# A trunk of two decoder layers on one core: all four output projections in panels of 1024 channels, with 60 of 136 chunk pairs by seven block products

## The chip, the core and the metric

The kernel runs on one core of a Trainium2 chip. The metric is the device time of one execution in microseconds, the median of several runs. The core has a matrix engine (TensorE, PE in the profile), three engines for elementwise work (VectorE, DVE; ScalarE, ACT; GpSimd, POOL) and a queue that issues the transfers (SyncE, SP). Each engine works through its own queue in order; semaphores hold an instruction until what it needs is there.

## The reference

256 tokens of 2048 channels pass through two layers, all in float32. Each layer is a mixer and a gated feed-forward block, both with a residual sum, and a last RMS norm closes the trunk:

```python
def reference(x, ...):
    h = x
    for i in range(DEPTH):                       # 2
        hn = rms_norm(h, mix_norm[i])
        if i % N_MIXERS == 0:
            h = h + retention_mixer(hn, ...)     # ends in y @ w_out, 4096 -> 2048
        else:
            h = h + moba_mixer(hn, ...)          # ends in o @ w_out, 2048 -> 2048
        h = h + conv_ffn(rms_norm(h, ffn_norm[i]), ...)   # ends in (silu(gate) * val) @ w_down, 5632 -> 2048
    return rms_norm(h, final_norm)
```

The four products that end the four blocks are the output projections. Their inner lengths are 4096, 5632, 2048 and 5632, that is 32, 44, 16 and 44 chunks of 128.

## The kernel before

**A product in three passes.** Each float32 factor is split into a high part (rounded to the fp32r type by ScalarE) and a low part (the difference, by VectorE); a product is high times high, high times low and low times high, three matmuls that are summed in PSUM. The split of the activations is stored with them (`hT`, `yT`, `oT`, `actT`: first 256 columns the high part, next 256 the low part). The weights come from memory in units of 1 MB (`raw`, 128 x 2048 elements, four buffers) and are split here, in parts of up to 1024 columns: ScalarE writes `wh` (L185) and VectorE writes `wl` (L186), four buffers each.

**The order of work.** The program is a list of parts. While TensorE works on part i, the parts up to i + 3 (`LOOKAHEAD`) may be split, and a buffer of `wh` is free again when TensorE is through with the part four places earlier. Work that hangs on a finished sum (residual sum, transposes, norms) is put some parts later with `after`. Within these rules a scheduler sets the order on each engine.

**Output projections before.** In `panel_a` a panel has 512 output channels; for each chunk and each half t of the tokens (128 tokens) three matmuls of 512 columns run (L265 to L267). A part is two chunks, 12 matmuls; two chunks with 1024 channels would be 24. Retention and block attention each take four such panels (`out_proj`, with `residual` adding the sum to `h`).

**Sevens and eights.** The first panel of each feed-forward projection is `panel_s`, with 1024 channels. Two chunks, two halves of the tokens and two halves of the channels make a product of 2 x 2 blocks by 2 x 2 blocks. As eight block products (an *eight* below) a pair is 8 x 3 = 24 matmuls in two parts, L354. As seven block products (a *seven*) it is 21 matmuls in four parts of 6, 3, 6 and 6 matmuls; for that the weights need three sums of blocks beside the blocks themselves (L203 to L205, on VectorE, in place in `raw`), and all that is used must be split: 3584 columns in place of 2048. The activations need sums of blocks too, the forms (L365 to L369, split at L185 and L186 into `hT`, which is free at that time). Seven of the 22 pairs of this panel are sevens, each with two eights between it and the next:

```python
SEVEN = list(range(3, NFB // 2, 3))
```

The sums of a seven are combined from four PSUM banks into `h` in `residual_s` (L739).

Of the kernel before, what the change touches and what calls it, by code (L numbers as in the profile page):

```python
# [28 lines left out]
SEVEN = list(range(3, NFB // 2, 3))  # L29
# [40 lines left out]

def build(tc, a, out):
# [27 lines left out]
    rB = cst.tile([P, S], F32, name="rB")  # L99
    rBq = cst.tile([P, S], F32, name="rBq")  # L100
# [53 lines left out]
    def issue_split(i):  # L154
# [3 lines left out]
        while state["dma"] <= min(u + 2, len(units) - 1):  # L158
            issue_dma(state["dma"])
            state["dma"] += 1  # L160
        wh = whi.tile([P, 1024], F32R, name="wh")
        wl = wlo.tile([P, 1024], F32R, name="wl")
        if i == 0:
            r = raws[u]

            def split(sl):
                split_to(wh[:, sl], wl[:, sl], r[:, sl])

            def rest():
                x_T(2, 2)  # L170
                split(slice(512, 1024))
                for _ in range(LOOKAHEAD):
# [21 lines left out]
    def split_b21(raw, wh, wl):  # L194
        split_to(wh[:, :512], wl[:, :512], raw[:, 1024:1536])

    def split_b11_b22(raw, wh, wl):
        b, h4, l4 = (v.rearrange("p (b n) -> p b n", n=512) for v in (raw, wh, wl))
        split_to(h4, l4, b[:, 0:4:3, :])

    def split_u4_u2(raw, wh, wl):
        b = raw.rearrange("p (b n) -> p b n", n=512)
        dve.tensor_tensor(b[:, 0:2, :], b[:, 0:4:3, :], b[:, 1:2, :].to_broadcast([P, 2, 512]), op=ALU.add)  # L203
        dve.tensor_tensor(b[:, 3, :], b[:, 0, :], b[:, 3, :], op=ALU.add)
        dve.tensor_tensor(b[:, 2, :], b[:, 3, :], b[:, 2, :], op=ALU.add)  # L205
        split_to(wh, wl, raw[:, 1024:])
# [50 lines left out]
    def panel_a(w, nk, n0, xT, done, before=None, split_last=0):  # L257


        box, late, items = {}, [], []  # L260

        def mm_t(t, k, c, wh, wl):
            acc, xt = box["acc"][t], xT[0]
# [5 lines left out]
        for k0 in range(0, nk, 2):  # L269
            def mm(wh, wl, k0=k0):  # L270
                if k0 == 0:
                    if before is not None:
                        before()
                    if split_last:
                        box["acc"] = [pacc.tile([P, 2, 512], F32, name="acc")[:, 0, :] for _ in range(2)]
                    else:
                        acc = pacc.tile([P, 2, 512], F32, name="acc")
                        box["acc"] = [acc[:, 0, :], acc[:, 1, :]]
                        box["tile"] = acc
                if k0 >= nk - 2 * split_last:  # L280
                    late.append((k0, wh, wl))
                    for c in range(2):
                        mm_t(0, k0 + c, c, wh, wl)
                else:
                    for c in range(2):
                        for t in range(2):
                            mm_t(t, k0 + c, c, wh, wl)
                if k0 == nk - 2:
                    if not split_last:
                        return finish(done, box["tile"])  # L290
                    done(box["acc"][0], 0)
                    for kl, wh, wl in late:
# [37 lines left out]
    def panel_s(w, nk, n0, xT, seven, forms, done):  # L330
# [3 lines left out]
        pairs = nk // 2  # L334
        acc, count, uses, items = {}, {}, {}, []
        for c in range(pairs):
            for b, m in (((2, 1), (3, 1), (4, 1), (1, 1), (5, 1), (6, 1), (7, 1)) if c in seven else
                         ((2, 2), (3, 2), (4, 2), (8, 2))):
                uses[b] = uses.get(b, 0) + 3 * m

        def bank(b):
            if b not in acc:
                if b in (2, 3, 4, 8):
                    acc[b] = paux.tile([P, 512], F32, name="aux")
                else:
                    i, j = (1, 6) if b in (1, 6) else (5, 7)
                    t = pacc.tile([P, 2, 512], F32, name="acc")
                    acc[i], acc[j] = t[:, 0, :], t[:, 1, :]
            return acc[b]
# [9 lines left out]
        def fs(s, i):  # L359
            return forms[:, 2 * s, i * P : (i + 1) * P], forms[:, 2 * s + 1, i * P : (i + 1) * P]  # L360

        def make_forms(s, k):

            a, f = ffn["p1"].tile([P, 2, S], F32, name="af", tag="bs"), ffn["p1"].tile([P, 4, P], F32, name="ff", tag="u1")
            dve.tensor_tensor(a, xT[0][:, k : k + 2, :S].bitcast(F32), xT[0][:, k : k + 2, S:].bitcast(F32), op=ALU.add)  # L365
            a4 = a.rearrange("p c (t m) -> p (c t) m", m=P)
            dve.tensor_tensor(f[:, 0:2, :], a4[:, 1:2, :].to_broadcast([P, 2, P]), a4[:, 0:4:3, :], op=ALU.subtract)
            dve.tensor_tensor(f[:, 2, :], a4[:, 0, :], f[:, 1, :], op=ALU.subtract)
            dve.tensor_tensor(f[:, 3, :], a4[:, 2, :], f[:, 2, :], op=ALU.subtract)  # L369
            f = f.rearrange("p f m -> p (f m)")  # L370
            split_to(forms[:, 2 * s, :], forms[:, 2 * s + 1, :], f)

        for c in range(pairs):
            k, last = 2 * c, c == pairs - 1
            ahead = (seven.index(c + 1), k + 2) if c + 1 in seven else None
            if c in seven:
                s = seven.index(c)

                def b21(wh, wl, k=k, last=last):
                    mul(2, xs(0, k + 1), wh[:, 0, :], wl[:, 0, :])  # L380
                    if last:
                        done(2, acc[2])

                def b11_b22(wh, wl, k=k, s=s, last=last):
                    mul(1, xs(0, k), wh[:, 0, :], wl[:, 0, :])
                    mul(3, fs(s, 3), wh[:, 1, :], wl[:, 1, :])
                    if last:
                        done(3, acc[3])

                def u4_u2(wh, wl, k=k, s=s, last=last):  # L390
                    mul(4, xs(1, k + 1), wh[:, 0, :], wl[:, 0, :])
                    mul(6, fs(s, 2), wh[:, 1, :], wl[:, 1, :])
                    if last:
                        for b in (1, 6, 4):
                            done(b, acc[b])

                def u1_u3(wh, wl, s=s, last=last):
                    mul(5, fs(s, 1), wh[:, 0, :], wl[:, 0, :])
                    mul(7, fs(s, 0), wh[:, 1, :], wl[:, 1, :])
                    if last:  # L400
                        for b in (5, 7):
                            finish(lambda acc, b=b: done(b, acc), acc[b])
# [598 lines left out]
```

## Time and profile before

| | |
|---|---|
| time, median of 3 runs | 2610.46 us (2609.38 to 2610.65) |
| profiled execution: its time, its span | 2611.6 us, 2609.8 us |
| busy share of the span: TensorE, VectorE, ScalarE | 99%, 67%, 51% |
| granted clock of TensorE, mean | 0.999 |
| chain that ended last | TensorE 97% |

The span is from the first to the last instruction of the profiled execution; its time also holds what lies around the program. A busy share is a mean over the whole span, and stages differ. The start to start distance of two instructions on an engine that never waits is what one costs; the durations in a row are longer, since neighbours overlap.

### The profile page before, as it was taken

The numbers are of one execution on the slowest core, as the hardware profiler recorded it, in microseconds if no ns is written. First come the engines' busy times: TensorE is split into PE (matmuls) and PEld (weight loads), VectorE is DVE, ScalarE is ACT, GpSimd is POOL, SyncE is SP. The second block draws the span as 40 slices with busy tenths as digits, with TensorE's granted clock in tenths as the row PEclk, the third lists the DMA queues.
The fourth block names the chain that finished last, engine by engine and source line by source line (L and its number), as shares of the span: only waits on it lengthen the run. The fifth ranks groups of instructions, "written<-read, shape, count | busy, mean of one in ns | idle before, by whom it ended". The sixth has DMA issues, their size and how long they took to land.

```text
span 2609.8 us, 33769 instructions
## 1 busy us (share of the span) xinstructions
PE 2595.9 (99%) x13456; PEld 2209.7 (85%) x13456; DVE 1758.9 (67%) x2247; ACT 1329.6 (51%) x1713; POOL 10.2 (0%) x24
## 2 busy tenths in 40 slices
PE   9999999999999999999999999999999999999998
PEld 7888888888888888888788888888888888888887
DVE  6666656564557777777975466665677777779764
ACT  5444444444445555555554454454555555555543
POOL 0000000000000000000000000000000000000000
PEclk9999999999999999999999999999999999999999
DMA  7655555555555555555555655555555565555563
GB/s 269 229 189 182 179 177 178 182 189 178 193 185 186 194 189 184 192 193 183 178 205 195 205 189 179 173 190 173 182 191 185 190 194 186 186 194 178 193 226 129
DMA packets 361149, 493.87 MB, mean 189 GB/s; under 512 B 8080, under 2 KB 258976, under 8 KB 360736
## 3 DMA queue, kind: packets, MB, share of 16 engines
q1 hardware_dynamic: 355248, 483.52, 56.1%
q10 hardware_dynamic: 5744, 8.20, 1.0%
q8 instruction: 105, 1.72, 0.3%
q14 instruction: 52, 0.43, 0.0%
HBM read 489.57 MB, written 5.27 MB: 190 GB/s over the span
## 4 chain that ended last, share of the span: by engine, by line
PE 97%; DVE 1%; issue 0%; ACT 0%; DMA 0%; SPq 0%; POOLq 0%; POOL 0%; DVEq 0%; ACTq 0%
PE acc L317 34%; PE acc L320 17%; PE acc L265 12%; PE acc L267 12%; PE acc L266 12%; PE aux L354 6%; PE acc L354 1%; PE aux L431 1%; PE aux L422 1%; PE aux L423 1%; PE aux L421 1%; DVE wl L186 0%; ACT wh L185 0%; PE aux L923 0%; DMA h<-in_x_dram 0%
## 5 line engine op out<-in xcount | busy, mean ns | idle before, releaser
L186 DVE TENSOR_TENSOR wl<-raw,wh 128x1024 fp32r<-128x1024 f32 (+1 forms) x941 | 1137.4, 1215 | 776.9 <-ACT wh L185 764.0
L185 ACT ACTIVATE wh<-raw 128x1024 fp32r<-128x1024 f32 (+1 forms) x941 | 985.3, 1053 | 1156.4 <-PE acc L317 477.3
L317 PE MATMUL acc<-hT,wh 128*128 128x512 f32 x3840 | 1209.6, 396 | 1.4 <-DVE hT L437 1.4
L320 PEld LDWEIGHTS acc<-hT,wl 128*128 128x128 f32 x3840 | 721.7, 188 | 170.1
L320 PE MATMUL acc<-hT,wl 128*128 128x256 f32 x3840 | 755.5, 278 | 0.0
L317 PEld LDWEIGHTS acc<-hT,wh 128*128 128x128 f32 x3840 | 587.0, 189 | 3.8 <-DVE hT L437 1.6
L265 PE MATMUL acc<-wh,hT 128*128 128x512 f32 x640 | 251.0, 392 | 0.7 <-DVE bs L567 0.7
L267 PE MATMUL acc<-wh,hT 128*128 128x512 f32 x640 | 249.3, 390 | 0.0
L266 PE MATMUL acc<-wl,hT 128*128 128x512 f32 x640 | 249.3, 390 | 0.0
L354 PE MATMUL aux<-wh,actT 128*128 128x512 f32 x536 | 170.2, 390 | 0.3 <-ACT wh L185 0.2
L718 DVE SCALAR_TENSOR_TENSOR t<-u,cw,t 128x256 f32<-128x256 f32 x352 | 146.8, 479 | 0.0
L267 PEld LDWEIGHTS acc<-wh,hT 128*128 128x128 f32 x640 | 120.2, 188 | 25.3
L265 PEld LDWEIGHTS acc<-wh,hT 128*128 128x128 f32 x640 | 120.2, 188 | 24.6 <-DVE bs L567 0.9
L266 PEld LDWEIGHTS acc<-wl,hT 128*128 128x128 f32 x640 | 120.3, 188 | 23.7
L265 PE MATMUL acc<-wh,actT 128*128 128x512 f32 x352 | 137.2, 390 | 0.0
L266 PE MATMUL acc<-wl,actT 128*128 128x512 f32 x352 | 137.1, 389 | 0.0
L267 PE MATMUL acc<-wh,actT 128*128 128x512 f32 x352 | 137.0, 389 | 0.0
L354 PEld LDWEIGHTS aux<-wh,actT 128*128 128x128 f32 x536 | 100.6, 188 | 22.0 <-ACT wh L185 1.9
L354 PE MATMUL aux<-wl,actT 128*128 128x512 f32 x268 | 105.7, 395 | 0.0
L265 PE MATMUL acc<-wh,yT 128*128 128x512 f32 x256 | 100.0, 390 | 0.0
L267 PE MATMUL acc<-wh,yT 128*128 128x512 f32 x256 | 99.7, 389 | 0.0
L266 PE MATMUL acc<-wl,yT 128*128 128x512 f32 x256 | 99.6, 389 | 0.0
(162 smaller groups left out, 1925.5 us busy)
## 6 DMA issues: line engine op xcount, KB each, us to landing
raw<-in_ffn_w_up_dram SPq DMA_DIRECT2D x176, 1024.0 KB, 5.1
raw<-in_ret_w_in_dram SPq DMA_DIRECT2D x93, 1024.0 KB, 5.2
raw<-in_ffn_w_down_dram SPq DMA_DIRECT2D x88, 1024.0 KB, 5.4
raw<-in_moba_w_qkv_dram SPq DMA_DIRECT2D x48, 1024.0 KB, 5.2
raw<-in_ret_w_out_dram SPq DMA_DIRECT2D x32, 1024.0 KB, 5.0
raw<-in_moba_w_out_dram SPq DMA_DIRECT2D x16, 1024.0 KB, 5.0
skewD<-tblD ACTq DMA_DIRECT2D x1, 3072.0 KB, 13.2
raw<-in_ret_w_in_dram SPq DMA_DIRECT2D x5, 512.0 KB, 9.1
```

What stands on the lines that cost most here:

```text
L185: act.activation(hi, src, AF.Copy)
L186: dve.tensor_tensor(lo, src, hi.bitcast(F32), op=ALU.subtract)
L265: pe.matmul(acc, lhsT=xh, rhs=wh[:, c, :], start=(k == 0), stop=False)
L266: pe.matmul(acc, lhsT=xh, rhs=wl[:, c, :], start=False, stop=False)
L267: pe.matmul(acc, lhsT=xl, rhs=wh[:, c, :], start=False, stop=(k == nk - 1))
L317: pe.matmul(acc[:, b, :], lhsT=wh[:, c, b * P : (b + 1) * P], rhs=xt[:, k, :], start=(k == 0), stop=False)
L320: pe.matmul(acc[:, b, S:], lhsT=wl[:, c, b * P : (b + 1) * P], rhs=xt[:, k, :S], start=False, stop=(k == KC - 1))
L354: pe.matmul(bank(b), lhsT=xs, rhs=ws, start=(n == 1), stop=(n == uses[b]))
L421: pe.matmul(dst, lhsT=lh, rhs=rh, start=start, stop=False)
L422: pe.matmul(dst, lhsT=lh, rhs=rl, start=False, stop=False)
L423: pe.matmul(dst, lhsT=ll, rhs=rh, start=False, stop=stop)
L718: dve.scalar_tensor_tensor(t[:, i, :], u[:, i, tap : tap + S], c[:, tap, b : b + 1], t[:, i, :], op0=ALU.mult, op1=ALU.add)
```

## The change

All four output projections become two panels of 1024 channels. Which pairs are sevens, in which order they come, and where forms are made or taken again is written out:

```python
FFN_SEQS = wide_seqs([5, 8, 10, 12, 14, 17, 19, 21], [1, 3, 7, 15], "AASSASFSASFSASFSAFAAAA")
RET_SEQS = wide_seqs([5, 7, 9, 11, 13, 15], [2, 4], "AASSASFSASFSAAAA")
MOB_SEQS = wide_seqs([3, 5, 7], [], "AASSSAAA")
```

The first list names the sevens of the first panel; in the string for the second panel, A is an eight, S a seven with a form that the first panel left in `hT`, F a seven whose form is made anew. That is 8 and 12 sevens of 22 and 22 pairs in each feed-forward projection, 6 and 8 of 16 and 16 in retention, 3 and 3 of 8 and 8 in block attention: 60 of 136, where 14 were before. The parts of a seven come in another order, and the sums of the weights are made with the first and the second part (L223, L228, L229). The sums of a seven stay in PSUM until they are added to `h`. `rB` and `rBq` become halves of one tile that also serves as a temporary. At the start, two parts are split ahead instead of three for the first eight parts, and transfers are issued one unit ahead instead of two. The end keeps its form: the last four parts finish the first 128 tokens ahead of the second 128.

```diff
-SEVEN = list(range(3, NFB // 2, 3))
...
+def wide_seqs(first, fresh, second):
+    n = len(second)
+    one = [(p, first.index(p) if p in first else None, p in first) for p in range(n)]
+    again, new = list(enumerate(first)), list(enumerate(fresh))
+    others = [p for p in range(n) if p not in first and p not in fresh]
+    two = []
+    for c in second:
+        if c == "A":
+            two.append((others.pop(0), None, False))
+        else:
+            slot, p = (again if c == "S" else new).pop(0)
+            two.append((p, slot, c == "F"))
+    return one, two
...
-        while state["dma"] <= min(u + 2, len(units) - 1):
+        while state["dma"] <= min(u + (1 if i < 8 else 2), len(units) - 1):
...
+    def split_b11_b22(raw, wh, wl):
+        b = blocks(raw)
+        split_to(blocks(wh), blocks(wl), b[:, 0:4:3, :])
+        dve.tensor_tensor(b[:, 0:2, :], b[:, 0:4:3, :], b[:, 1:2, :].to_broadcast([P, 2, 512]), op=ALU.add)
+
     def split_b21(raw, wh, wl):
...
+        b = blocks(raw)
+        split_to(wh[:, :512], wl[:, :512], b[:, 2, :])
         dve.tensor_tensor(b[:, 3, :], b[:, 0, :], b[:, 3, :], op=ALU.add)
         dve.tensor_tensor(b[:, 2, :], b[:, 3, :], b[:, 2, :], op=ALU.add)
...
-            while state["split"] <= min(i + LOOKAHEAD if i else 0, n - 1):
+            ahead = 0 if i == 0 else 2 if i < 8 else LOOKAHEAD
+            while state["split"] <= min(i + ahead, n - 1):
...
+        def opens(i):
+
+            if i == 0:
+                if before is not None:
+                    before()
+                begin()
+            if i == sevens[0]:
+                begin_sevens()
+            if i + 2 < len(seq) and seq[i + 2][2]:
+                make_forms(seq[i + 2][1], 2 * seq[i + 2][0])
+
+        def seven(i, k, s):
+            def b11_b22(wh, wl):
+                opens(i)
+                mul(1, xs(0, k), wh[:, 0, :], wl[:, 0, :])
+                mul(3, fs(s, 3), wh[:, 1, :], wl[:, 1, :])
+                give()
+
+            def b21(wh, wl):
+                mul(2, xs(0, k + 1), wh[:, 0, :], wl[:, 0, :])
+                give()
+
+            def u1_u3(wh, wl):
+                mul(5, fs(s, 1), wh[:, 0, :], wl[:, 0, :])
+                mul(7, fs(s, 0), wh[:, 1, :], wl[:, 1, :])
+                give()
+
+            def u4_u2(wh, wl):
+                mul(4, xs(1, k + 1), wh[:, 0, :], wl[:, 0, :])
+                mul(6, fs(s, 2), wh[:, 1, :], wl[:, 1, :])
+                ends()
+
+            return [(split_b11_b22, b11_b22), (split_b21, b21), (0, u1_u3), (1, u4_u2)]
...
-    def out_proj(w, nk, xT, g0, use_r, j0=0):
+    def out_proj(w, seqs, xT, temps, g0, use_r):
...
+        emit(panel_s(w, 0, xT, seqs[0], temps, residual_s(0, temps)))
+        emit(panel_s(w, 1024, xT, seqs[1], temps,
+                     residual_s(2, temps, lambda: [transpose_first(i) for i in range(2)], rest)))
...
-        emit(panel_s(wd, NFB, 0, actT, SEVEN, hT, residual_s(0, then)))
-        if last:
-            emit(panel_a(wd, NFB, 2 * 512, actT, last_done(2)))
-            emit(panel_a(wd, NFB, 3 * 512, actT, last_half, split_last=3))
-        else:
-            out_proj(wd, NFB, actT, g_next, use_next, j0=2)
+        if not last:
+            return out_proj(wd, FFN_SEQS, actT, temps_ffn, g_next, use_next)
...
+        emit(panel_s(wd, 0, actT, FFN_SEQS[0], temps_ffn, residual_s(0, temps_ffn)))
+        emit(panel_s(wd, 1024, actT, FFN_SEQS[1], temps_ffn, residual_s(2, temps_ffn, last=last_bank), end=4,
+                     before=gains_first))
```

The first place is VectorE's queue between sevens in the feed-forward projection of layer 0. Before, late in the panel with sevens (`wl` at L186 is the low part of a split, the three lines on `raw` are the sums of a seven):

```order
L186 TENSOR_TENSOR wl<-raw,wh 128x512
L186 TENSOR_TENSOR wl<-raw,wh 128x1024
L203 TENSOR_TENSOR raw<-raw 128x1024
L204 TENSOR_TENSOR raw<-raw 128x512
L205 TENSOR_TENSOR raw<-raw 128x512
L186 TENSOR_TENSOR wl<-raw,wh 128x1024 x6
L186 TENSOR_TENSOR wl<-raw,wh 128x512
```

The same engine after, in the second panel, in the stretch S A S F of the string (`wl` is now L208, `hT<-ff` the split of a form):

```order
L208 TENSOR_TENSOR wl<-raw,wh 128x1024 x5
L208 TENSOR_TENSOR wl<-raw,wh 128x512
L223 TENSOR_TENSOR raw<-raw 128x1024
L208 TENSOR_TENSOR hT<-ff,hT 128x512
L228 TENSOR_TENSOR raw<-raw 128x512
L208 TENSOR_TENSOR wl<-raw,wh 128x1024
L229 TENSOR_TENSOR raw<-raw 128x512
L208 TENSOR_TENSOR wl<-raw,wh 128x1024 x2
L208 TENSOR_TENSOR wl<-raw,wh 128x512
L223 TENSOR_TENSOR raw<-raw 128x1024
L228 TENSOR_TENSOR raw<-raw 128x512
L229 TENSOR_TENSOR raw<-raw 128x512
```

Before, eight splits stand between one group of sums and the next, four of them those of two eights; after, the seven behind the eight has its sums interleaved with the split of a form, and the next group of sums stands only three splits behind, with no eight between.

The second place is VectorE's queue where the first panel of that projection ends and the next one begins. Before (`m` are copies of the sums of a seven in SBUF, made by ScalarE):

```order
L739 TENSOR_TENSOR h<-aux,h 128x512
L186 TENSOR_TENSOR wl<-raw,wh 128x1024 x2
L739 TENSOR_TENSOR h<-h,m_10977 128x512
L739 TENSOR_TENSOR m_10979<-m_10979,m_10977 128x512
L186 TENSOR_TENSOR wl<-raw,wh 128x1024
L739 TENSOR_TENSOR m_10977<-m_10979,m_10996 128x512
L186 TENSOR_TENSOR wl<-raw,wh 128x1024
L739 TENSOR_TENSOR h<-h,m_10977 128x512
L739 TENSOR_TENSOR m_10979<-m_10979,m_10994 128x512
L186 TENSOR_TENSOR wl<-raw,wh 128x1024
L739 TENSOR_TENSOR h<-h,m_10979 128x512
L739 TENSOR_TENSOR m_10996<-m_10977,m_10994 128x512
```

After (`acc` and `aux` are PSUM):

```order
L558 TENSOR_TENSOR rBs<-acc,m 128x512
L208 TENSOR_TENSOR wl<-raw,wh 128x1024
L558 TENSOR_TENSOR h<-h,rBs 128x512
L223 TENSOR_TENSOR raw<-raw 128x1024
L558 TENSOR_TENSOR m<-acc,m 128x512
L208 TENSOR_TENSOR wl<-raw,wh 128x512
L558 TENSOR_TENSOR h<-h,m 128x512
L228 TENSOR_TENSOR raw<-raw 128x512
L558 TENSOR_TENSOR rBs<-acc,rBs 128x512
L229 TENSOR_TENSOR raw<-raw 128x512
L558 TENSOR_TENSOR h<-h,rBs 128x512
L208 TENSOR_TENSOR wl<-raw,wh 128x1024 x3
```

The sums into `h` stood between splits of plain parts; now the last of them stand between the weight sums of the second panel's first seven.

## Rows read from the trace of the kernel before

**Rows 1.** The page of the profile: the busy time of each engine, the granted clock in 40 slices, and the share of the span that each engine has in the chain that ended last.

```profile
PE 2595.9 (99%) x13456; PEld 2209.7 (85%) x13456; DVE 1758.9 (67%) x2247; ACT 1329.6 (51%) x1713; POOL 10.2 (0%) x24
...
PEclk9999999999999999999999999999999999999999
...
PE 97%; DVE 1%; issue 0%; ACT 0%; DMA 0%; SPq 0%; POOLq 0%; POOL 0%; DVEq 0%; ACTq 0%
```

**Rows 2.** Busy time of each engine by stretch: in the feed-forward projection of layer 0 the pairs around the first three sevens, the rest of that panel, and what stands behind it (a panel of 512 channels and a part of the next). Columns: stretch and its length, then busy us (instructions) for PE, PEld, DVE, ACT, POOL, the granted clock, DMA share and GB/s.

```profile
1262.00:1302.00 40.00, 39.35 (x167) 30.66 (x166) 38.30 (x53) 23.18 (x26) 0.00 (x0) 1.00 0.48 164
1302.00:1364.00 62.00, 62.00 (x272) 50.31 (x271) 46.21 (x46) 30.43 (x35) 0.00 (x0) 1.00 0.56 201
1364.00:1480.00 116.00, 116.00 (x525) 96.25 (x525) 64.63 (x69) 54.37 (x69) 0.00 (x0) 1.00 0.60 201
```

**Rows 3.** TensorE in order of time, in the last panel of 512 channels: start, duration, engine, line, operation. The second row is the 24th matmul behind the first.

```profile
2574.26 0.39 PE L265 MATMUL acc<-wh,actT 128*128 128x512 f32 x1
...
2579.70 0.39 PE L265 MATMUL acc<-wh,actT 128*128 128x512 f32 x1
```

**Rows 4.** Stretches of the matmuls of the panel with sevens alone (L354): first 24 matmuls at a time (48 where the length is 10.88) of layer 0, where the second, fourth, fifth and sixth of these stretches hold the first, second, third and fourth seven; then that panel as a whole in both layers, 507 matmuls. Columns as in Rows 2, PE and PEld alone.

```profile
1256.78:1262.22 5.44, 5.44 (x25) 4.50 (x24) 1.00 0.35 139
1262.22:1268.56 6.34, 6.13 (x25) 4.35 (x24) 1.00 0.16 19
1268.56:1279.44 10.88, 10.88 (x49) 9.01 (x48) 1.00 0.75 281
1279.44:1285.91 6.47, 6.11 (x26) 4.35 (x24) 1.00 0.20 40
...
1296.79:1302.75 5.96, 5.88 (x25) 4.33 (x24) 1.00 0.34 89
...
1313.63:1319.23 5.60, 5.60 (x26) 4.43 (x24) 1.00 0.49 165
...
1245.87:1363.92 118.05, 117.39 (x507) 94.20 (x507) 1.00 0.52 183
2363.50:2481.56 118.06, 117.41 (x507) 94.22 (x507) 1.00 0.52 183
```

**Rows 5.** VectorE in order of time between two sevens, where it is without idle time (idle time stands in brackets at the end of a row): start, duration, engine, line, operation. What an instruction costs is the distance to the next start.

```profile
1274.25 0.29 DVE L368 TENSOR_TENSOR ff<-af,ff 128x128 f32<-128x128 f32 x1
1274.58 0.29 DVE L369 TENSOR_TENSOR ff<-af,ff 128x128 f32<-128x128 f32 x1
1274.78 1.22 DVE L186 TENSOR_TENSOR wl<-raw,wh 128x1024 fp32r<-128x1024 f32 x1
1275.92 0.69 DVE L186 TENSOR_TENSOR hT<-ff,hT 128x512 fp32r<-128x512 f32 x1
1276.52 1.22 DVE L203 TENSOR_TENSOR raw<-raw 128x1024 f32<-128x1024 f32 x1
1277.66 0.69 DVE L365 TENSOR_TENSOR af<-actT 128x512 f32<-128x512 f32 x1
1278.26 0.69 DVE L204 TENSOR_TENSOR raw<-raw 128x512 f32<-128x512 f32 x1
1278.86 0.42 DVE L367 TENSOR_TENSOR ff<-af 128x256 f32<-128x256 f32 x1
1279.20 0.69 DVE L205 TENSOR_TENSOR raw<-raw 128x512 f32<-128x512 f32 x1
```

**Rows 6.** The same view at a later seven: the three additions one behind the other, each of which reads what the one before it wrote.

```profile
1324.50 1.23 DVE L203 TENSOR_TENSOR raw<-raw 128x1024 f32<-128x1024 f32 x1
1325.76 0.69 DVE L204 TENSOR_TENSOR raw<-raw 128x512 f32<-128x512 f32 x1
1326.49 0.69 DVE L205 TENSOR_TENSOR raw<-raw 128x512 f32<-128x512 f32 x1
```

**Rows 7.** VectorE in a panel of 512 channels of the retention output projection: same columns.

```profile
660.93 1.23 DVE L186 TENSOR_TENSOR wl<-raw,wh 128x1024 fp32r<-128x1024 f32 x1 [1.49 <-ACT wh L185]
663.65 1.23 DVE L186 TENSOR_TENSOR wl<-raw,wh 128x1024 fp32r<-128x1024 f32 x1 [1.49 <-ACT wh L185]
```

**Rows 8.** The start by stretch, columns as in Rows 2.

```profile
5.00:9.00 4.00, 1.35 (x8) 0.71 (x6) 1.19 (x3) 2.61 (x7) 0.00 (x0) 1.00 1.00 326
9.00:13.00 4.00, 3.96 (x13) 3.33 (x14) 2.92 (x5) 3.94 (x10) 0.00 (x0) 0.57 1.06 369
...
20.00:36.00 16.00, 16.00 (x99) 14.05 (x98) 12.15 (x20) 11.24 (x20) 0.70 (x1) 1.00 1.05 386
36.00:60.00 24.00, 23.32 (x109) 19.24 (x109) 17.19 (x24) 10.65 (x12) 0.00 (x0) 1.00 0.56 185
```

**Rows 9.** The end: the last matmul on TensorE, and on VectorE the first and the last instruction of the first half of the tokens (rows two and three) and the first and the last one of the second half (rows four and five).

```profile
2601.23 0.39 PE L267 MATMUL acc<-wh,actT 128*128 128x512 f32 x1
...
2597.58 0.76 DVE L790 TENSOR_TENSOR h<-acc,h 128x256 f32<-128x256 f32 x2 [4.48 <-PE acc L267]
...
2600.93 0.48 DVE L806 TENSOR_SCALAR h<-hg,rf 128x512 f32<-128x512 f32 x1
2601.66 0.76 DVE L790 TENSOR_TENSOR h<-acc,h 128x256 f32<-128x256 f32 x2 [0.25 <-PE acc L267]
...
2605.01 0.48 DVE L806 TENSOR_SCALAR h<-hg,rf 128x512 f32<-128x512 f32 x1
```

**Rows 10.** DMA issues of the page: count, size, median us from issue to landing.

```profile
raw<-in_ffn_w_down_dram SPq DMA_DIRECT2D x88, 1024.0 KB, 5.4
```

More of the change, by code (lines that the diff above doesn't have):

```diff
@@ L171, in rest @@
                 split(slice(512, 1024))
-                for _ in range(LOOKAHEAD):
+                for _ in range(2):
                     issue_split(state["split"])
@@ L328, in panel_b, with panel_s, begin, begin_sevens @@
         return items
[L330 to L349, printed above, removed]
+    def panel_s(w, n0, xT, seq, temps, done, end=None, before=None):
+        acc, count, uses, items, late = {}, {}, {}, [], []
+        sevens = [i for i, (_, slot, _) in enumerate(seq) if slot is not None]
+        for _, slot, _ in seq:
+            for b, m in (((2, 8), (4, 8), (3, 8), (8, 8)) if slot is None else
+                         ((1, 1), (3, 1), (2, 1), (5, 1), (7, 1), (4, 1), (6, 1))):
+                uses[b] = uses.get(b, 0) + (6 if m == 8 else 3)
+        def begin():
+            wide[0] = True
+            spare.clear()
+            for b in (2, 3, 8, 4):
+                acc[b] = paux.tile([P, 512], F32, name="aux")
+        def begin_sevens():
+            spare.clear()
+            for b0, b1 in ((1, 6), (5, 7)):
+                t = pacc.tile([P, 2, 512], F32, name="acc")
+                acc[b0], acc[b1] = t[:, 0, :], t[:, 1, :]
         def mul(b, x, wh, wl):
@@ new lines, in panel_s, with ends, eight, mm @@
+        left = [4 * len(sevens) + 2 * (len(seq) - len(sevens))]
+        def ends():
+            if not left[0]:
+                wide[0] = False
+            give()
+        def eight(i, j, k):
+            def mm(wh, wl):
+                if j == 0:
+                    opens(i)
+                c = 2 * i + j
+                to_go = 2 * len(seq) - c
+                order = ((2, 0, 0), (3, 0, 1), (8, 1, 1), (4, 1, 0)) if c == 0 else \
+                        ((2, 0, 0), (4, 1, 0), (3, 0, 1), (8, 1, 1))
+                if end is not None and to_go <= end:
+                    late.append((k + j, wh, wl))
+                    order = ((2, 0, 0), (3, 0, 1))
+                for b, t, n in order:
+                    mul(b, xs(t, k + j), wh[:, n, :], wl[:, n, :])
+                if end is not None and to_go == 1:
+                    give()
+                    for b, t, n in ((4, 1, 0), (8, 1, 1)):
+                        for kl, hl, ll in late:
+                            mul(b, xs(t, kl), hl[:, n, :], ll[:, n, :])
+                        give()
+                ends()
+            return mm
@@ new lines, in counted, with f, aux_tile @@
+        def counted(mm):
+            def f(wh, wl):
+                left[0] -= 1
+                mm(wh, wl)
+            return f
+        for i, (pair, slot, _) in enumerate(seq):
+            k = 2 * pair
+            mms = [(j, eight(i, j, k)) for j in range(2)] if slot is None else seven(i, k, slot)
+            items.append((unit_s(w, k, n0), [(part, counted(mm)) for part, mm in mms]))
+        return items
+    wide, spare = [False], []
+    def aux_tile():
+        if not wide[0]:
+            return paux.tile([P, 512], F32, name="aux")
+        if not spare:
+            t = pacc.tile([P, 2, 512], F32, name="acc")
+            spare.extend([t[:, 1, :], t[:, 0, :]])
+        return spare.pop()
```

280 lines of the change are left out of this document (114 added, 166 removed).

## The prediction

> **What bounds the kernel now.** I read the page first. TensorE is busy 99% of the span at full clock, and the chain that ended last lies on it for 97% [rows 1]. Whoever removes matmuls can therefore gain. VectorE's 67% is a mean, so I then cut the trace into stretches. Around the first three sevens of the feed-forward projection VectorE is busy 38.30 of 40 us, later in that panel 46.21 of 62, and behind it 64.63 of 116 [rows 2]. So in this kernel the second engine is already at its limit where sevens stand close to other work. The reader should see in these three rows that the spare time of VectorE lies in the stretches without sevens, and that is where the change puts its sevens.
>
> **What is removed.** One 512-column matmul costs 5.44 / 24 = 0.2267 us, start to start [rows 3]. A seven has 21 instead of 24. 60 - 14 = 46 more sevens remove 138 matmuls, 138 x 0.2267 = 31.3 us. The sevens of before also have waits: the panel takes 118.05 us where 507 x 0.2267 = 114.9 would do, 3.1 us in each layer, 6.2 in all, and these are seen one by one: 24 matmuls take 6.34, 6.47 and 5.96 us around the first three sevens in place of 5.44 [rows 4]. With another order of pairs these waits go; what comes in their place is counted below from zero. Credit: 37.5 us.
>
> **What is added.** VectorE's instructions cost, start to start, 1.14 us for 1024 columns, 0.60 for 512, 0.34 for 256 and 0.33 for 128 [rows 5]. An eight needs two splits of 1024, 2.28 us, beside 5.44 us of TensorE. A seven needs three splits and one sum of 1024, one split and two sums of 512: 4 x 1.14 + 3 x 0.60 = 6.36 us, beside 21 x 0.2267 = 4.76 us. Where a sum directly follows the sum that it reads, it comes 1.26 and 0.73 us behind in place of 1.14 and 0.60, 0.12 more each [rows 6]. A seven thus overdraws VectorE by 1.6 us, an eight gives 3.2. What may be kept in stock is small: four buffers of `wh` and `wl`, so VectorE is at most three parts ahead.
>
> So the question is how the sevens stand. In a first panel they alternate with eights, and from the program's order the sums are: feed-forward, from its first to its last seven, 48 instructions of 1024 columns, 35 of 512, 16 small, 7 dependent pairs, 54.7 + 21.0 + 5.3 + 0.8 = 81.8 us against 378 matmuls or 85.7 us. Retention is 50.1 against 54.4, block attention 24.2 against 23.8. No wait worth counting; I take zero for the first panels (bounds 0 and 2 us, two waits of the size of [rows 4] at most).
>
> In the second panels two or three sevens stand together with one eight between. I count what stands in VectorE's queue from the second part of the panel's first seven (up to there VectorE is ahead) to the last split of the last seven of the dense run, and TensorE's time for the same parts but the last one, which is 6 matmuls:
> - Retention, 8 sevens and 2 eights: 34 x 1.14 + 28 x 0.60 + 1.0 = 56.6 us; TensorE 210 x 0.2267 = 47.6. Surplus 9.0.
> - Feed-forward of layer 0, 11 sevens and 3 eights: 48 x 1.14 + 41 x 0.60 + 3.0 = 82.3; TensorE 297 x 0.2267 = 67.3. Surplus 15.0.
> - Block attention, 3 sevens: 10 x 1.14 + 11 x 0.60 = 18.0; TensorE 57 x 0.2267 = 12.9. Surplus 5.1.
> - Feed-forward of layer 1, the same as layer 0 with four multiplications by the final gain: 84.7 against 67.3. Surplus 17.4.
>
> The 512-column instructions in these counts hold the last three sums into `h` of the first panel, and the 512-column and small ones the forms made or split in the run; the two orders shown above are such places. Surplus 46.5 us, and 36 dependent pairs x 0.12 = 4.3: 50.8 us. A surplus on VectorE is a wait of TensorE, since TensorE can't start a part without its split, and behind a waiting matmul stand all the others. The eights inside are already in the count, so no cover is left. The lead at the start of a run could be one split and two sums larger (1.14 + 2 x 0.60 = 2.34 us in each of four runs): then 41.4. I take 50.8, because at the first seven of a second panel VectorE comes from the sums into `h`, not from idle time.
>
> **What moves without a price.** ScalarE's splits and transfers: a unit lasts 4.8 to 5.4 us on TensorE and lands 5.4 us behind its issue [rows 10], issued two units ahead; bytes and number stay. At the start, TensorE is without a gap from 20 to 36 us and lacks 0.7 us up to 60 [rows 8]; splitting two ahead in place of three can win that 0.7 or lose about one split, so -0.7 to +1.2, taken as 0. At the end, the last matmul starts at 2601.23 and the second half's chain on VectorE runs from 2601.66 to 2605.01 [rows 9]; it is the same chain after, 0 (bounds 0.6 either way, one 512-column pass). At the seams between stages, eight chunks in place of four are transposed behind the last sum; VectorE idles 1.49 us in each 2.72-us part of plain work [rows 7], which covers these; up to +3 if not.
>
> **Sum.** 50.8 - 37.5 = +13.3 us. The profiled execution has 2611.6 us, 1.1 over the median of 2610.46; carried to the median, 2610.5 + 13.3 = 2624 us. With the larger lead it is 2614, with the dear ends of the other edits (2.0 + 1.2 + 0.6 + 3) 2631: 2614 to 2631 for this case.
>
> **A rule beside it.** From [rows 5] 512 more columns cost 0.54 us, so a 1024-column pass is 1.08 us of columns and 0.06 fixed. The Trainium skill (VectorE: DVE Perf Modes, section Mode 1×) says that a two-input float32 operation gives one result per cycle of 0.96 GHz, 1.067 us for 1024 columns: the trace's 1.14 is dearer. By the page's figure alone the 210,944 columns of the four runs would be 219.7 us (an estimate), the surplus 24.6, and the change 13 us faster, so the fixed part decides the sign.
>
> **Rivals.** *The fixed part hides* (faster). If VectorE took instructions that are all ready at the rate of their columns, 288 instructions x 0.06 = 17.3 us and the 4.3 of dependent pairs would go: surplus 29.2, change -8.3, 2602 us. It decides from 13.3 / 245.9 = 5.4% less VectorE time on. Against it: the starts in [rows 5] are already those of an engine without idle time.
> *The lead is larger and the first panels give some of it back* (no change): surplus near 38 to 42, 2606 to 2615. For it: the sevens of before wait less from one to the next [rows 4].
> *No surplus at all*: the full credit, 2573 us. Against it are the first two sevens, which wait with two eights between [rows 4].
> *The clock falls.* After the start's pause, TensorE busy 1.35 of 4 us, the next 4 us run at a granted 0.57, the lower of the two levels of 1.2 and 2.4 GHz [rows 8]. In the dense runs TensorE pauses within most sevens. At the lower level a seven is 9.5 us, not 6.6; were it so for 9 of the 33 sevens, 9 x 2.9 = 26 more: 2650 us. Against it: sevens with 0.5 to 1.0 us of waits left the clock at 1.00 [rows 4]. The Trainium skill (TensorE: Matmul & The Clock Gate, section A second HAM failure mode) tells of short pauses between groups of matmuls that let the clock go down and up; by that rule this rival holds, and no row here has such pauses at a stretch.
>
> **How the numbers follow.** This measurement tells 0.2%, 5.2 us, from no change. Chances: the forecast 0.66, the clock 0.08, the larger lead 0.12, the fixed part 0.11, no surplus 0.03. Slower is 0.66 + 0.08, less a little of the forecast's low end: 0.73; same 0.13; faster 0.14. The range leaves out the case without surplus and parts of the fixed-part and clock cases, and takes in the bounds: 2600 to 2640.
>
> **What the trace would show.** Right: in the second panels VectorE busy over 95% over some 60 to 100 us, ended waits of TensorE by the split of VectorE, 15 to 18 us more than the matmuls' own time per feed-forward projection, 9 to 10 in retention, 5 in block attention; first panels without waits. Wrong: VectorE starts closer than 1.14 us, or idle time of VectorE within the runs, or a granted clock below 1.00 there, or new waits at the start, the seams or the end.

## The result and the profile after

The changed kernel takes 2634.16 us, median of 4 runs (2632.53 to 2634.70), against 2610.56 us (2609.38 to 2610.78) of the kernel before in the same series: ratio 1.0090, 95% interval 1.0073 to 1.0108. It is 23.6 us slower. The forecast was 2624 us, slower by 13.3. The direction and the mechanism came out as forecast, the size did not: 2634 lies in the stated 2600 to 2640, but 3 us above the 2614 to 2631 that the prediction gave for its own case.

The page of the changed kernel, rows that answer to [rows 1]:

```profile
PE 2582.2 (98%) x13318; PEld 2183.4 (83%) x13318; DVE 2013.0 (77%) x2629; ACT 1415.0 (54%) x1827; POOL 10.2 (0%) x24
...
PE   9999999999899999999998999999999999999988
...
PE 83%; DVE 13%; issue 2%; ACT 1%; DMA 0%; POOL 0%; ACTq 0%; SPq 0%; POOLq 0%; DVEq 0%
```

TensorE has 138 matmuls less (13456 to 13318) and is no longer without gaps: its row has 8s in place of 9s in the 11th, the 22nd and the last but one slice (the last one had an 8 before too). VectorE has 254 us more, and the chain that ended last now lies on it for 13% of the span, before for 1%.

The matmuls of the new panels alone (L364), by panel, in the order retention first and second panel, feed-forward of layer 0, block attention, feed-forward of layer 1, columns as in [rows 4]:

```profile
571.05:657.20 86.15, 83.86 (x367) 68.59 (x367) 1.00 0.53 182
657.20:753.20 96.00, 86.78 (x361) 66.29 (x359) 1.00 0.58 191
1246.10:1361.60 115.50, 115.01 (x505) 94.41 (x506) 1.00 0.55 188
1361.60:1494.30 132.70, 120.05 (x493) 91.66 (x491) 0.99 0.56 186
1787.60:1832.00 44.40, 42.48 (x183) 34.06 (x183) 1.00 0.47 154
1832.00:1880.10 48.10, 43.72 (x184) 33.62 (x182) 1.00 0.66 215
2374.00:2489.40 115.40, 114.87 (x504) 94.33 (x505) 1.00 0.58 195
2489.40:2622.30 132.90, 120.12 (x493) 93.43 (x491) 0.97 0.46 151
```

What a panel waits is its length, less its matmuls at 0.2267 us [rows 3], less what else stands among them: transposes at 0.1 us, and in two first panels the last matmuls of the mixer (nine of 512 columns in retention, 2.0 us, and 24 short ones in block attention, 2.6 us). The fourth row has 12 sevens and 10 eights, 492 matmuls or 111.5 us, and 1.6 us of transposes: 132.7 - 113.1 = 19.6 us of waits. In the same way the second panels wait 12.8 (retention), 19.6, 5.3 (block attention) and 21.4 us, 59.1 in all, the first panels 0.3, 1.2, 0.3 and 1.2, together 3.0. The time went into the second panels, where the sevens stand close.

Who is waited for, TensorE's waits (engine, tile and line, releaser: us in total, times, longest):

```profile
PE aux L364 <- ACT wh L207: 19.3, 27, 2.0
PE acc L364 <- ACT wh L207: 12.0, 17, 1.2
PE acc L364 <- DVE wl L208: 3.8, 5, 0.8
PE aux L364 <- DVE wl L208: 1.7, 3, 0.7
```

Most are put down to ScalarE's half of a split. But ScalarE is busy 46 of 85 us there (first row below, columns as in [rows 2]) and waits itself for VectorE's sums; the engine that is full is VectorE. Its stretches in the second panels, of the feed-forward projection of layer 0, of layer 1, of retention and of block attention:

```profile
1380.00:1465.00 85.00, 73.75 (x295) 55.28 (x295) 81.85 (x95) 46.32 (x52) 0.00 (x0) 0.98 0.52 174
2505.00:2595.00 90.00, 77.49 (x308) 58.93 (x307) 87.03 (x104) 47.29 (x54) 0.00 (x0) 0.96 0.51 170
680.00:722.00 42.00, 37.38 (x156) 28.70 (x155) 39.70 (x42) 23.43 (x27) 0.00 (x0) 1.00 0.53 176
1836.00:1866.00 30.00, 26.54 (x112) 20.37 (x111) 29.73 (x35) 18.59 (x26) 0.00 (x0) 1.00 0.53 173
```

96, 97, 95 and 99% busy. Inside, VectorE in order of time behind the stretch that the section on the change shows (start, duration, engine, line, idle time before it in brackets), and below it the ScalarE row at the same place:

```profile
1419.13 0.68 DVE L229 TENSOR_TENSOR raw<-raw 128x512 f32<-128x512 f32 x1
1421.02 2.96 DVE L208 TENSOR_TENSOR wl<-raw,wh 128x1024 fp32r<-128x1024 f32 x3 [1.21 <-ACT wh L207]
1423.90 1.22 DVE L223 TENSOR_TENSOR raw<-raw 128x1024 f32<-128x1024 f32 x1
1425.15 0.69 DVE L228 TENSOR_TENSOR raw<-raw 128x512 f32<-128x512 f32 x1
1425.88 0.69 DVE L229 TENSOR_TENSOR raw<-raw 128x512 f32<-128x512 f32 x1
1426.49 4.25 DVE L208 TENSOR_TENSOR wl<-raw,wh 128x1024 fp32r<-128x1024 f32 x4
1430.66 1.22 DVE L223 TENSOR_TENSOR raw<-raw 128x1024 f32<-128x1024 f32 x1
...
1419.93 2.53 ACT L207 ACTIVATE wh<-raw 128x1024 fp32r<-128x1024 f32 x3 [1.98 <-DVE raw L229]
```

A row with x3 or x4 holds several splits under the shape of the first: the three from 1421.02 to 1423.90 are two of 1024 columns and one of 512, 2 x 1.14 + 0.60 = 2.88 us. So the costs are those of [rows 5, 6]: the sum at L228 comes 1.25 us behind L223, L229 0.73 behind that. From one L223 to the next, a seven behind a seven, are 6.76 us, where TensorE needs 4.76. Not in the prediction is the 1.21 us of rest: ScalarE, which works in order, waits for L229; when that is done, VectorE has nothing else in reach and waits for ScalarE's pass of about 1.06 us. The same wait comes back smaller in the 6.76 us, which are 0.16 more than 4 x 1.14 + 3 x 0.60 + 2 x 0.12 = 6.60. Behind L229 the first split starts at 1426.49 and the second one 1.29 us later in place of 1.14, when the ScalarE pass that waited for L229 is through:

```profile
1427.78 2.36 DVE L208 TENSOR_TENSOR wl<-raw,wh 128x1024 fp32r<-128x1024 f32 x2
...
1426.69 2.53 ACT L207 ACTIVATE wh<-raw 128x1024 fp32r<-128x1024 f32 x3 [0.39 <-DVE raw L229]
```

### The profile page after: what moved, and what is told of

Same layout as the page of the kernel before. It is cut to its first block, busy times and chain, and to the rows that moved or that the text cites. A ratio compares the mean times of both kernels' runs of the same rounds, so it can differ in the third digit from the quotient of the medians.

```text
span 2630.8 us, 34125 instructions
## 1 busy us (share of the span) xinstructions
PE 2582.2 (98%) x13318; PEld 2183.4 (83%) x13318; DVE 2013.0 (77%) x2629; ACT 1415.0 (54%) x1827; POOL 10.2 (0%) x24
## 4 chain that ended last, share of the span: by engine, by line
PE 83%; DVE 13%; issue 2%; ACT 1%; DMA 0%; POOL 0%; ACTq 0%; SPq 0%; POOLq 0%; DVEq 0%
PE acc L322 34%; PE acc L325 17%; PE aux L364 11%; DVE wl L208 6%; PE acc L288 6%; PE acc L289 6%; PE acc L290 6%; PE acc L364 2%; DVE raw L223 2%; ACT wh L207 1%; DVE raw L228 1%; DVE raw L229 1%; DVE h L558 1%; DVE hT L208 1%; PE aux L481 1%
## 5 line engine op out<-in xcount | busy, mean ns | idle before, releaser
L207 ACT ACTIVATE wh<-raw 128x1024 fp32r<-128x1024 f32 (+1 forms) x1033 | 1056.5, 1034 | 1078.6 <-PE acc L322 469.8
L208 DVE TENSOR_TENSOR wl<-raw,wh 128x1024 fp32r<-128x1024 f32 (+1 forms) x1033 | 1216.0, 1191 | 548.7 <-ACT wh L207 533.0
L364 PE MATMUL aux<-wh,actT 128*128 128x512 f32 x928 | 307.9, 393 | 12.0 <-ACT wh L207 12.0
L288 PE MATMUL acc<-wh,hT 128*128 128x512 f32 x640 | 251.0, 392 | 0.0
L290 PE MATMUL acc<-wh,hT 128*128 128x512 f32 x640 | 249.3, 390 | 0.0
L364 PEld LDWEIGHTS aux<-wh,actT 128*128 128x128 f32 x928 | 175.0, 189 | 54.1 <-ACT wh L207 18.4
L364 PE MATMUL aux<-wl,actT 128*128 128x512 f32 x464 | 181.6, 391 | 1.7 <-DVE wl L208 1.7
L364 PE MATMUL acc<-wh,hT 128*128 128x512 f32 x360 | 135.5, 404 | 12.0 <-ACT wh L207 12.0
L289 PEld LDWEIGHTS acc<-wl,hT 128*128 128x128 f32 x640 | 120.3, 188 | 23.6
L364 PE MATMUL aux<-wh,yT 128*128 128x512 f32 x344 | 114.4, 393 | 4.7 <-ACT wh L207 4.7
L364 PEld LDWEIGHTS aux<-wl,actT 128*128 128x128 f32 x464 | 87.3, 188 | 22.6 <-DVE wl L208 4.7
L364 PEld LDWEIGHTS acc<-wh,hT 128*128 128x128 f32 x360 | 69.3, 192 | 34.0 <-ACT wh L207 20.5
L827 ACT ACTIVATE t<-u,cw 128x256 f32<-128x256 f32 x176 | 95.2, 589 | 0.2
L680 DVE TENSOR_TENSOR bs<-acc,bs 128x512 f32<-128x512 f32 x120 | 82.1, 684 | 0.0
```

The costliest lines, as they stand in the source:

```text
L207: act.activation(hi, src, AF.Copy)
L208: dve.tensor_tensor(lo, src, hi.bitcast(F32), op=ALU.subtract)
L288: pe.matmul(acc, lhsT=xh, rhs=wh[:, c, :], start=(k == 0), stop=False)
L289: pe.matmul(acc, lhsT=xh, rhs=wl[:, c, :], start=False, stop=False)
L290: pe.matmul(acc, lhsT=xl, rhs=wh[:, c, :], start=False, stop=(k == nk - 1))
L364: pe.matmul(acc[b], lhsT=xs, rhs=ws, start=(n == 1), stop=(n == uses[b]))
```

## Experiments

In each expectation, theory A is that of the prediction: VectorE's work for sevens that stand too close ends last. The kernel before took 2610.6 to 2611.8 us in the three series of runs, so a difference between two kernels of different series is uncertain by about 1 us.

**Sevens apart.** The same panels and code, other strings:

```diff
-FFN_SEQS = wide_seqs([5, 8, 10, 12, 14, 17, 19, 21], [1, 3, 7, 15], "AASSASFSASFSASFSAFAAAA")
-RET_SEQS = wide_seqs([5, 7, 9, 11, 13, 15], [2, 4], "AASSASFSASFSAAAA")
-MOB_SEQS = wide_seqs([3, 5, 7], [], "AASSSAAA")
+FFN_SEQS = wide_seqs([5, 8, 10, 12, 14, 17, 19, 21], [], "AASASASASASASASASAAAAA")
+RET_SEQS = wide_seqs([5, 7, 9, 11, 13, 15], [], "AASASASASASASAAA")
+MOB_SEQS = wide_seqs([4, 6], [], "AASASAAA")
```

> In the second panels every seven is followed by an eight, none by another seven, and no form is made anew: 48 sevens instead of 60 (8 and 8 in each feed-forward projection, 6 and 6 in retention, 2 and 2 in block attention). Theory A, the waits come of VectorE's work standing too close: a seven and an eight together take VectorE about 6.76 + 2 x 1.14 = 9.0 us (the period of sevens that follow each other in the changed kernel, and two plain splits) and TensorE 4.76 + 5.44 = 10.2 us, so the 59.1 us of waits in the second panels fall to 2 to 6, at the price of 12 sevens less (12 x 0.68 = 8.2 us): 2634 - 55 + 8 = 2587, from 2578 to 2592, faster than the kernel before by 18 to 32 us. Theory B, each seven costs a fixed wait however it stands (hand-over between its four parts, or banks): 23 sevens of the second panels at 59.1 / 35 = 1.7 us is 39 us, so 2634 - 20 + 8 = 2622, from 2612 to 2632. Theory C, the waits come of the granted clock after pauses: waits per seven as they are wherever sevens remain, as B.

Measured: 2588.88 us against 2611.84 of the kernel before, ratio 0.9913 (0.9897 to 0.9930). With 12 sevens less the kernel is 45 us faster than the changed one, and faster than the kernel before by 23 us. The second panels of this kernel, in the order of the table above:

```profile
659.10:744.40 85.30, 84.05 (x367) 68.15 (x365) 1.00 0.64 220
1352.80:1469.80 117.00, 115.63 (x505) 93.97 (x503) 1.00 0.61 210
1809.60:1853.40 43.80, 42.89 (x186) 34.61 (x186) 1.00 0.60 203
2461.80:2578.10 116.30, 115.03 (x505) 94.15 (x504) 1.00 0.49 173
```

The second row has 504 matmuls, 114.3 us, and 1.6 of transposes: 1.1 us of waits in place of 19.6. The four rows together wait 4.5 us. Theory B, a fixed wait for each seven, falls: for the 24 sevens of these panels it asks for 24 x 1.7 = 41 us. Theory C, the granted clock, asked for as much and falls with it. What costs is where the sevens stand, not how many there are.

**Without the sums.**

```diff
-        dve.tensor_tensor(b[:, 0:2, :], b[:, 0:4:3, :], b[:, 1:2, :].to_broadcast([P, 2, 512]), op=ALU.add)
...
-        dve.tensor_tensor(b[:, 3, :], b[:, 0, :], b[:, 3, :], op=ALU.add)
-        dve.tensor_tensor(b[:, 2, :], b[:, 3, :], b[:, 2, :], op=ALU.add)
```

> The changed kernel without the three sums of weight blocks (L223, L228, L229), so the products that need them are computed from the plain blocks. Everything else stays: order, parts, splits, banks, transfers. Theory A: VectorE's time for a seven falls from 6.6 to 6.8 us to about 3 x 1.14 + 0.60 = 4.0 us, under TensorE's 4.76, and nearly all of the 59.1 + 3.7 us of waits go: 2634 - 60 = 2574, from 2570 to 2582. Theory B, the waits come of the four-part hand-over, of banks or of buffers: 2620 to 2634.

Measured: 2575.28 us against 2611.84, ratio 0.9861 (0.9846 to 0.9876). All eight panels wait 0.3 to 0.4 us each, 2.8 in all, which is little more than the rounded prices of this count leave. Order, parts, banks, forms and transfers are the same, so none of these makes the waits; the sums do. The run takes out VectorE's work and ScalarE's wait for it together; the next one adds work alone, in the sevens of the second panels (`dense`).

**One more pass.**

```diff
...
+        if dense[0]:
+            dve.tensor_tensor(scr.tile([P, 512], BF16, name="junk"), b[:, 0, :], b[:, 1, :], op=ALU.add)
...
```

> The changed kernel with one more VectorE operation of 512 columns (an extra sum that nobody reads) in each seven of the second panels, 35 in all. Theory A, VectorE is the bound in the runs of sevens, so what is added there is added to the end: 35 x 0.60 = 21 us, less what the first seven of a run and the three sevens of block attention hide (4 to 6 us): +14 to +21, 2648 to 2655. Theory B, VectorE's rest in the runs (about 2.3 us in each of three) and the hand-overs are what is waited for and VectorE is not full: +0 to +6, 2634 to 2640.

Measured: 2647.37 us against 2611.84, ratio 1.0135 (1.0120 to 1.0150), 13.2 us above the changed kernel. That is just under the 14 to 21 of A and more than twice the 6 at B's upper end. VectorE at one seven of it, the added pass at L233:

```profile
1432.53 0.68 DVE L230 TENSOR_TENSOR raw<-raw 128x512 f32<-128x512 f32 x1
1433.13 0.68 DVE L233 TENSOR_TENSOR junk<-raw 128x512 bf16<-128x512 f32 x1
1433.74 0.68 DVE L231 TENSOR_TENSOR raw<-raw 128x512 f32<-128x512 f32 x1
```

Each pass costs the 0.60 us assumed, 21 in all. But it stands between two sums of which one reads the other, as in the rows above, and the 0.12 us of such a pair falls away: in the second panels 40 sums start directly behind the sum that they read in the changed kernel, 11 in this one, 29 x 0.12 = 3.5 us less. That leaves 17.5 us of more work for VectorE. The waits of the second panels grow by 10.0 (59.1 to 69.1), and 4.7 us went into VectorE's rests, which shrink from 8.9 to 4.2 us over the four dense runs, all gaps counted. The other 2.8 us may lie at the first and the last seven of a run, where there is lead; that is not shown. VectorE is the limit, but not without slack.

**The sums on GpSimd.** The three additions as above on `nc.gpsimd` instead of `dve`.

> The changed kernel with the three sums of weight blocks of every seven on GpSimd in place of VectorE. No row of either trace shows what such a sum costs on GpSimd; the nearest is 128 x 2 elements in 0.69 us against 0.06 to 0.1 us fixed on VectorE. Theory A1, GpSimd works beside VectorE and at no less than half its speed (at most 4.7 us for the three sums of a seven): VectorE's part of a seven is 4.0 us, TensorE's 4.76, and the 62 us of waits nearly go: 2572 to 2585. Theory A2, GpSimd is three times slower (7.0 us a seven) and becomes the bound of the runs: 7.0 - 4.76 = 2.2 us for each of the 33 sevens of the dense runs, 2572 + 75 = 2647, from 2635 to 2660. Theory A3, a sum on GpSimd stops VectorE's two-input passes while it lasts: then a seven costs VectorE 4.0 + 4.7 to 7.0 = 8.7 to 11 us, 2 to 4.4 us more than now for each of 33, and first panels wait too: 2700 to 2780. The Trainium skill (SBUF - State Buffer, section SBUF: two separate sides) says that VectorE and GpSimd lock a pair of ports against each other for whole instructions; by that A3 holds.

Measured: 2778.46 us against 2611.84, ratio 1.0639 (1.0623 to 1.0655), as A3 has it. GpSimd over two sevens and the start of a third, and below VectorE beside the first of them:

```profile
1479.88 2.38 POOL L223 TENSOR_TENSOR raw<-raw 128x1024 f32<-128x1024 f32 x1 [6.50 <-DVE wl L208]
1482.34 1.63 POOL L228 TENSOR_TENSOR raw<-raw 128x512 f32<-128x512 f32 x1
...
1489.42 2.77 POOL L223 TENSOR_TENSOR raw<-raw 128x1024 f32<-128x1024 f32 x1 [3.74 <-DVE wl L208]
...
1499.33 2.77 POOL L223 TENSOR_TENSOR raw<-raw 128x1024 f32<-128x1024 f32 x1 [3.56 <-DVE wl L208]
...
1480.29 2.53 DVE L208 TENSOR_TENSOR wl<-raw,wh 128x512 fp32r<-128x512 f32 x1 [0.48 <-ACT wh L207]
1482.74 1.78 DVE L208 TENSOR_TENSOR hT<-ff,hT 128x512 fp32r<-128x512 f32 x1
```

Two 512-column passes of VectorE take 2.53 and 1.78 us in place of 0.69; both end within 0.6 us behind the GpSimd sum that ran when they began (1482.26 and 1483.97). A seven to the next is 9.9 us. The granted clock is 0.978 in the mean of this profile, against 0.997 in that of the changed kernel, so some of its matmuls ran at the lower level; what that adds was not separated. The Trainium skill (SBUF — State Buffer, section SBUF: two separate sides) tells of an exclusive lock on a shared pair of ports, held for a whole instruction; the trace agrees, with these two passes.

**More sevens with a place or two where they meet.**

```diff
-FFN_SEQS = wide_seqs([5, 8, 10, 12, 14, 17, 19, 21], [], "AASASASASASASASASAAAAA")
+FFN_SEQS = wide_seqs([5, 8, 10, 12, 14, 17, 19, 21], [1, 3], "AASASASSASASSAFASAFAAA")
```

> The spread kernel with 10 sevens instead of 8 in the second panel of each feed-forward projection, 52 in all, in the order A A S A S A S S A S A S S A F A S A F A A A: two places where a seven follows a seven, and two forms made anew. Theory A in its average form: over the panel VectorE has less to do than TensorE (10 x 6.4 + 12 x 2.3 + two forms of about 2.5 = 97 us against 10 x 4.76 + 12 x 5.44 = 113), so nothing waits and 4 more sevens give 4 x 0.68 = 2.7 us: 2586. Theory A in its local form: what counts is the lead at hand, a seven behind a seven waits 6.4 - 4.76 = 1.6 us or more (2.0 in the changed kernel), and an eight behind them makes nothing of it good: 4 such places, +6.4 to +8, less 2.7: 2593 to 2594. I take the local form for half of it: 2590, from 2585 to 2595.

Measured: 2596.01 us against 2610.89, ratio 0.9942 (0.9930 to 0.9955), 7.1 us more than the spread kernel, where 2.7 less were to be won. Its second panels of the feed-forward projections wait 5.6 and 6.0 us, those of the spread kernel 1.1 and 2.0. At the four places where a seven follows a seven, the second one waits 2.59, 1.45, 2.52 and 1.45 us. Over the first of these panels VectorE is busy 110.44 of 119.70 us, TensorE 116.45, so VectorE has less to do; that does not help, since the program keeps no more than three parts in stock. The local form of A holds, and its price was rather low.

**A deeper stock.**

```diff
-LOOKAHEAD = 3
+LOOKAHEAD = 4
...
-    wraw = ctx.enter_context(tc.tile_pool(name="wraw", bufs=4))
-    whi = ctx.enter_context(tc.tile_pool(name="whi", bufs=4))
-    wlo = ctx.enter_context(tc.tile_pool(name="wlo", bufs=4))
+    wraw = ctx.enter_context(tc.tile_pool(name="wraw", bufs=3))
+    whi = ctx.enter_context(tc.tile_pool(name="whi", bufs=5))
+    wlo = ctx.enter_context(tc.tile_pool(name="wlo", bufs=5))
```

> The changed kernel with four parts split ahead instead of three: five buffers each for the two halves of a split instead of four, and three instead of four for the units from memory, to make room. Theory A, VectorE's work is the bound in each run: a deeper lead is won once in a run, at most one part, 1.2 to 2.3 us in each of four runs: -2 to -8, 2626 to 2632. Theory B, the shallow lead is what makes a seven behind a seven wait, since four parts of a seven don't fit into a lead of three: then half or more of the 59 us go: 2595 to 2608. Were three buffers for units too few, a new wait on transfers would show in the trace and the run would say less.

Measured: 2626.15 us against 2610.89, ratio 1.0057 (1.0043 to 1.0071), 8.0 less than the changed kernel. The waits of all panels are 54.5 us in place of 62.1. The first seven of a second panel waits 0.0 in place of 0.7; sevens far into a run wait 1.95 to 1.99 us as before. What a deeper stock wins, it wins for the most part at the first two sevens of a run, as A has it. The waits on transfers that the expectation names as a danger are there, on ScalarE, where the changed kernel has none on these two tensors:

```profile
ACT wh L207 <- DMA raw<-in_ffn_w_down_dram: 13.4, 8, 3.2
...
ACT wh L207 <- DMA raw<-in_ret_w_out_dram: 4.3, 2, 2.3
```

They lie in the first panels and ahead of and behind the dense runs, not in them, and no wait of TensorE in the eight panels is put down to a transfer; so they do not hide a gain of the size that B asks for.

**The start alone**, in the kernel before and taken out of the changed kernel:

```diff
-        while state["dma"] <= min(u + 2, len(units) - 1):
+        while state["dma"] <= min(u + (1 if i < 8 else 2), len(units) - 1):
...
-            while state["split"] <= min(i + LOOKAHEAD if i else 0, n - 1):
+            ahead = 0 if i == 0 else 2 if i < 8 else LOOKAHEAD
+            while state["split"] <= min(i + ahead, n - 1):
```

> The kernel before with nothing of the change but the start: two parts split ahead instead of three for the first eight parts, transfers one unit ahead instead of two. The prediction's step said 0 (bounds -0.7 to +1.2): 2610.5. The one profiled execution of the changed kernel reached its first matmul of the retention projection 3.1 us earlier than the one of the kernel before (571.0 against 574.2), which by itself says -3.1: 2607.5. In the profiles of the spread, the sumless and the dosed kernel, which start in the same way, that matmul comes at 573.0, 572.8 and 573.8, that is 0.4 to 1.4 earlier. I take -1: 2609.5, from 2607.5 to 2611.5.

Measured: 2610.18 us against 2610.89, ratio 0.9997 (0.9988 to 1.0006): no change that can be told.

> The changed kernel with the start of the kernel before. If the new start is worth 3.1 us, 2637; if it is worth 0 to 1, 2634 to 2635. I take 2635, from 2633 to 2638.

Measured: 2635.92 us against 2610.89, ratio 1.0095 (1.0081 to 1.0108), which overlaps the changed kernel's 1.0090. The 3.1 us that the changed kernel's profile showed at the start are scatter of one execution. The stretch from 9 to 13 us of the changed kernel, of the spread kernel and of the kernel before with the new start, the same program there in all three:

```profile
9.00:13.00 4.00, 4.00 (x27) 1.00 1.08 373
```

```profile
9.00:13.00 4.00, 4.00 (x15) 0.58 1.06 370
```

```profile
9.00:13.00 4.00, 4.00 (x17) 0.63 1.06 367
```

The columns are TensorE alone, then the granted clock: 1.00 in one execution, 0.58 and 0.63 in two others. The first matmul of the retention projection comes at 571.0, 573.0 and 572.4 us, in the profile of the kernel before at 574.2.

**One sum for all.** 2610.5, less 0.68 us for each seven over 14, less 6.2 us of waits of before, and plus the waits that the eight panels of each kernel show:

| kernel | sevens | waits in its panels | sum | measured |
|---|---|---|---|---|
| changed | 60 | 62.1 | 2635.1 | 2634.2 |
| apart | 48 | 7.5 | 2588.7 | 2588.9 |
| without sums | 60 | 2.8 | 2575.8 | 2575.3 |
| one more pass | 60 | 72.2 | 2645.2 | 2647.4 |
| sums on GpSimd | 60 | 205.5 | 2778.5 | 2778.5 |
| more sevens | 52 | 17.6 | 2596.1 | 2596.0 |
| deeper stock | 60 | 54.5 | 2627.5 | 2626.2 |

All agree within 2.2 us. Nothing outside the waits and the matmul count is needed. In this count matmuls at the lower clock stand among the waits.

## Why the prediction came out as it did

- **Credit, 37.5 us: right.** The sum above rests on it, and the kernel without sums, with 2.8 us of waits, is 36.6 us faster than the kernel before (34.7 by the sum).
- **VectorE's costs: right.** 1.14, 0.60 and the 0.12 more for a sum that reads the one ahead of it are in the rows after. The rival in which the fixed part hides has fallen.
- **Surplus of the second panels, 50.8 us: right in kind, too small by 8.3.** Retention 12.8 for 9.0, feed-forward 19.6 and 21.4 for 15.0 and 17.4, block attention 5.3 for 5.1; to these forecasts come the 4.3 us of dependent pairs, which the prediction has in one sum for all four. The step that failed is the count of VectorE's queue as if it never paused in a run. Its rests, without the 0.03 us that belong to dependent sums, are about 2 us in each of the three long runs, 6 in all, the largest the 1.21 us above. The small wait behind L229, 0.15 us, stands in 15 places of the four runs, 2.3 us. Both are waits for a ScalarE pass, the largest and the small ones for a pass that itself waits for L229, and together they have the size of the 8.3 us. In block attention, with 0.27 us of gaps in 30, the count was right to a few tenths. The rests are seen, not undone by an experiment; the added pass showed that 4.7 us more work fit into them.
- **First panels, 0 (bounds 0 and 2): 3.0 us.** 1.4 of these are there without the sums too, 0.3 to 0.4 a panel, little more than the rounded prices of the count leave; the other 1.6 lie in the two feed-forward projections, 0.8 each, within the bounds.
- **Start 0: right**, though the profile of the changed kernel by itself spoke against it. **Tail 0: right.** Rows that answer to [rows 9], the last matmul and the last instruction of VectorE:

```profile
2622.11 0.39 PE L364 MATMUL aux<-wh,actT 128*128 128x512 f32 x1
...
2625.95 0.48 DVE L881 TENSOR_SCALAR h<-hg,rf 128x512 f32<-128x512 f32 x1
```

3.84 us apart, before 3.78.
- **The larger lead, and no surplus: wrong.** One part more of stock, which the deeper kernel has, is worth 8 us; the changed kernel does not have it.
- **The clock falls: seen, without a price that shows.** In two of the dense runs, those of the feed-forward projections, the clock fell for some microseconds behind a pause (TensorE alone by stretch, its busy time, clock third from the end; then its matmuls):

```profile
1400.00:1403.00 3.00, 1.61 (x4) 0.84 0.35 142
1403.00:1406.00 3.00, 3.00 (x10) 0.60 0.06 11
1406.00:1409.00 3.00, 2.37 (x12) 1.00 0.87 298
...
1403.68 0.63 PE L364 MATMUL acc<-wh,hT 128*128 128x512 f32 x1
1404.10 0.63 PE L364 MATMUL aux<-wh,actT 128*128 128x512 f32 x1
```

Busy 1.61 of 3 us, then matmuls 0.43 us apart, the lower of the two levels. The two runs have some 20 such matmuls, 4 us if nothing hid them. But they stand in stretches that wait for VectorE, and the changed kernel with the old start shows what they cost: in its profile the clock fell five times in these two panels in place of three, with 35 such matmuls, and the panels are as long, 132.70 and 132.90 us:

```profile
1363.20:1495.90 132.70, 121.21 (x493) 92.82 (x492) 0.97 0.55 185
2491.00:2623.90 132.90, 121.38 (x494) 94.46 (x492) 0.96 0.45 152
```

The Trainium skill's rule on short pauses (TensorE: Matmul & The Clock Gate, section A second HAM failure mode) agrees with the fall as far as these rows go; the panels of the changed kernel as a whole stayed at 0.97 to 1.00.

So 13.3 + 8.3 + 3.0 = 24.6, against 23.6 measured. The prediction's signs of being wrong name idle time of VectorE within the runs and a granted clock below 1.00 there: both came, the first with a price, the second without one that shows.

## What to carry to other kernels

A trade of work from one engine to another has to be balanced over a stretch no longer than the stock between the two, not over a panel: 48 sevens with an eight between them gave 23 us, 52 with four places where they meet 15, and 60 packed close lost 24. When a queue is counted as a bound, add the rests that its dependences through a third engine force on it. And a difference of a few microseconds in one profile at the start is no effect until runs show it.

## What was not expected of the hardware

- A sum on GpSimd holds up VectorE's two-input passes: 2.53 us for 0.69, with GpSimd at 2.71 us for 1024 columns (mean of 60), where VectorE takes 1.22. Moving work to the idle engine cost 144 us here, the lower granted clock of that run included.
- The same start shows granted clocks of 1.00, 0.58 and 0.63 from 9 to 13 us in three executions.
